# Decoder trunk on one core: score products of row halves and quarters issued in turn, and two gates ahead of the first two branches

## The chip, the core and the metric

The kernel runs on one core of a Trainium2 chip. The metric is device time in microseconds of one execution of the whole program, as the median of several runs. Engines are named as the profile names them: PE (TensorE, matmuls and transposes; PEld are its weight loads), DVE (VectorE), ACT (ScalarE), POOL (GpSimd) and SP (SyncE, which issues the DMAs).

## The reference, cut to what matters

Two layers over one sequence of 256 tokens, width 1024, all float32. Each layer projects the normalised input once, runs four causal mixers (4 query heads of 64 each) on slices of that projection, merges the four results through sigmoid gates, and adds a convolutional feed-forward part.

```python
h = rms_norm(x, norm1_g)
u = h @ w_in
yA = dsa_mixer(...)
yB = moba_mixer(...)
yC = nsa_mixer(...)
yD = swa_mixer(...)
m = sum(sigmoid(gate_n) * (y_n @ w_branch[n]) for n in range(4))
x = x + m @ w_out
x = x + conv_ffn(rms_norm(x, norm2_g), ...)
```

Here `u` holds the columns of the four mixers (2612 in all) and, behind them, the four gates of 1024 columns each. At 256 tokens the mixers are dense masked attention with different masks. A (DSA) has one shared key head and keeps for each query the 64 keys that an indexer scores highest: eight index heads of 32, `I[t,s] = sum_h w[t,h] relu(q_idx[t,h] . k_idx[s])`. B (MoBA) has four key heads and is plain causal here. C (NSA) adds three attentions with a gate each: over 15 compressed blocks (a small MLP makes them), over selected blocks and over a window; at this length the last two are causal attentions with keys of their own. D (SWA) has a window of 128, two key heads and a sink per head.

## The kernel before, in words

**Dense products.** Weights come in chunks of up to 1 MB through three `raw` buffers on SP's queue, in the order of the list `plan` (lines 380 to 435). ACT rounds each piece to `hi` (line 467), DVE computes `lo`, what is left of it (line 477); four buffers each. Activations are split in the same way (`ahi`, `alo`), and a dense product is three PE passes, hi by hi, lo by hi and hi by lo (`macs`, lines 492 to 525), for two tiles of 128 tokens, into the `mm` banks of PSUM. There are four `mm` banks, two `sc` banks (scores) and two `tr` banks (transposes and small products).

**Order of the work.** Everything is unrolled. Each piece of work is a generator ("stream") that asks for an engine, for results and for buffers of rings; `Flow.run` (line 139) is a planner that always lets the stream go on whose request can start first by its clocks, and emits its instructions then. So the order in which each engine's queue holds its instructions is fixed when the program is built, by the costs in `Eng.cost` (lines 180 to 206). For a float32r matmul of n columns line 189 says 0.417 n + 2 ns, doubled while PE's clock in the plan is below 6.7 us. Where two streams can start at the same time the priority decides (a smaller number first; the mixers' are `PRIO`, line 396, A 4, B 19, C 7, D 21, and the main stream's is 40).

**The main stream** (`main`, lines 1233 to 1394) goes through a layer in one order: projections in the column order `PORDER` = A, B, D, C (line 397), then for each branch n = 0 to 3 its gate (two halves of 512 columns, `gate_out` applies the tanh) and its branch product, and then the output projection and the feed-forward part. Between gate 0 and branch 0 stand two small products for C's compression (`hidden`, lines 1019 to 1029), which wait for C's first steps; they run on four column strips of the array with `P.side = 4`. For branches 0 to 2 both gate halves come first and then both branch halves; for branch 3 they alternate. `branch_out` waits for that mixer's result, turned by `y_T` (line 581), which main spawns one branch at a time; `merge` (line 1115) multiplies it with the gate and adds it to `mg`. Gates lie in four places of `slotP` in turn.

**The mixers** (`dsa`, `moba`, `nsa`, `swa`, lines 775 to 1009) are streams of their own that main spawns as their projections end, and they fill PE between main's instructions. One set of buffers, `prep_r` (line 259), is held by one mixer at a time while it normalises, rotates and transposes its queries and keys: A from line 777 to 830, B from 867 to 881, D from 888 to 903, C from 912 to 1005, the last across the compression product. A and B and D ask for it as an ACT request, C as a DVE request. POOL's instructions on `rB`, `rC` and `rD` are the power in each mixer's query norm.

**The score products** that the change is about are the only matmuls that use a part of the array's rows. `attend` (lines 634 to 708) runs for one tile t of 128 queries, nk = 128 (t + 1) keys and four heads of 64: heads 0 and 2 lie in rows 0 to 63, heads 1 and 3 in rows 64 to 127. There are ten attends in a layer (A, B, D, and C twice; t = 0 and 1):

```python
for par in range(2):
    ...
    for hh in range(2):
        te = P.matmul(sc[:, hh * nk:hh * nk + nk], qT[b:b + 64, hh, ...], kT[b:b + 64, ...])
    fl.spawn(attend_max(...), 8)
```

Each half takes one `sc` bank by a request of its own (lines 641 and 645). `indexer` (lines 836 to 864) does the same for the eight index heads of A in four row quarters r4 of 32 rows, one `sc` bank and one request per quarter (lines 840 to 847), followed by a Relu on ACT and two accumulations on DVE.

## Time and profile before

| | us |
|---|---|
| three runs | 877.33, 877.55, 881.88 |
| median of the runs | 877.55 |
| the profiled execution's own time | 881.64 |
| its span, first to last instruction | 879.8 |
| PE in flight | 874.4 |
| DVE busy | 667.9 |
| ACT busy | 526.3 |
| POOL busy | 34.3 |

The profile is one execution; times in its views count from the start of the span. A matmul's time there is its flight: matmuls are pipelined, so the next one starts before the flight of the one before has ended, and the cost of an instruction is read from start to start. The timeline merges neighbours of one kind into one line with their count; most instructions carry line 212, the helper that records them, so groups are told apart by their tiles (output<-inputs).

### The profile page before, as it was taken

The numbers are of one execution on the slowest core, as the hardware profiler recorded it, in microseconds if no ns is written. First come the engines' busy times: TensorE is split into PE (matmuls) and PEld (weight loads), VectorE is DVE, ScalarE is ACT, GpSimd is POOL, SyncE is SP. The second block draws the span as 40 slices with busy tenths as digits, with TensorE's granted clock in tenths as the row PEclk, the third lists the DMA queues.
The fourth block names the chain that finished last, engine by engine and source line by source line (L and its number), as shares of the span: only waits on it lengthen the run. The fifth ranks groups of instructions, "written<-read, shape, count | busy, mean of one in ns | idle before, by whom it ended". The sixth has DMA issues, their size and how long they took to land.

```text
span 879.8 us, 14193 instructions
## 1 busy us (share of the span) xinstructions
PE 874.4 (99%) x5491; PEld 766.2 (87%) x5491; DVE 667.9 (76%) x1301; ACT 526.3 (60%) x895; POOL 34.3 (4%) x31
## 2 busy tenths in 40 slices
PE   9999999999999999999999999999999999999998
PEld 8979887788889999988898888787888999999886
DVE  4779888956768999884457997968476699899642
ACT  5655465555457887764455465646545598888431
POOL 0111002000000000000001111000000000000000
PEclk9999999999999999999999999999999999999999
DMA  7627364235555555555554264542356455565560
GB/s 266 237 87 240 96 239 145 83 127 174 192 176 179 200 191 192 193 168 193 170 172 168 85 205 144 193 144 97 120 184 222 144 192 195 194 201 192 178 215 25
DMA packets 103413, 149.90 MB, mean 170 GB/s; under 512 B 4072, under 2 KB 62258, under 8 KB 103346
## 3 DMA queue, kind: packets, MB, share of 16 engines
q1 hardware_dynamic: 103346, 149.00, 50.6%
q8 instruction: 43, 0.70, 0.3%
q14 instruction: 24, 0.20, 0.1%
HBM read 147.94 MB, written 1.05 MB: 169 GB/s over the span
## 4 chain that ended last, share of the span: by engine, by line
PE 98%; ACT 0%; DMA 0%; SPq 0%; DVE 0%; issue 0%; DVEq 0%
PE mm L212 82%; PE sc L212 8%; PE tr L212 8%; DMA rn<-in_norm_g_dram 0%; ACT f L212 0%; ACT L212 0%; SPq L240 0%; ACT hi L212 0%; DVE x L212 0%; DVEq L1429 0%
## 5 line engine op out<-in xcount | busy, mean ns | idle before, releaser
L212 DVE TENSOR_TENSOR lo<-raw,hi 128x1024 fp32r<-128x1024 f32 (+2 forms) x280 | 328.1, 1177 | 117.2 <-ACT hi L212 113.3
L212 ACT ACTIVATE hi<-raw 128x1024 fp32r<-128x1024 f32 (+2 forms) x280 | 283.3, 1022 | 170.7 <-PE mm L212 143.1
L212 PE MATMUL mm<-hi,ahi 128*128 128x512 f32 (+4 forms) x480 | 178.1, 377 | 0.0
L212 PE MATMUL mm<-hi,alo 128*128 128x512 f32 (+4 forms) x480 | 172.3, 365 | 0.0
L212 PE MATMUL mm<-ahi,hi 128*128 128x256 f32 x640 | 152.3, 279 | 0.0
L212 PE MATMUL mm<-alo,hi 128*128 128x256 f32 x640 | 152.0, 278 | 0.0
L212 PEld LDWEIGHTS mm<-ahi,hi 128*128 128x128 f32 x640 | 120.6, 188 | 0.1
L212 PEld LDWEIGHTS mm<-alo,hi 128*128 128x128 f32 x640 | 120.6, 188 | 0.1
L212 PE MATMUL mm<-lo,ahi 128*128 128x512 f32 (+4 forms) x480 | 118.3, 370 | 0.0
L212 PEld LDWEIGHTS mm<-hi,ahi 128*128 128x128 f32 x480 | 90.7, 189 | 14.9 <-issue 2.7
L212 PEld LDWEIGHTS mm<-hi,alo 128*128 128x128 f32 x480 | 90.8, 189 | 11.2
L212 PEld LDWEIGHTS mm<-lo,ahi 128*128 128x128 f32 x480 | 82.9, 188 | 13.8 <-issue 1.7
L212 PE MATMUL mm<-hi,slotQ 128*128 128x512 f32 x352 | 89.9, 395 | 0.0
L212 PE MATMUL mm<-ahi,lo 128*128 128x256 f32 x640 | 88.1, 278 | 0.0
L212 PEld LDWEIGHTS mm<-ahi,lo 128*128 128x128 f32 x640 | 80.2, 188 | 0.0
L212 PEld LDWEIGHTS mm<-hi,slotQ 128*128 128x128 f32 x352 | 66.1, 188 | 15.3
L212 ACT ACTIVATE f<-f,col 128x256 f32<-128x256 f32 x88 | 48.1, 593 | 14.5 <-DVE f L212 14.0
L212 PE MATMUL mm<-lo,slotQ 128*128 128x512 f32 x176 | 48.7, 395 | 0.0
L212 ACT ACTIVATE f<-f,nmx 128x128 f32<-128x128 f32 (+1 forms) x80 | 35.4, 445 | 9.6 <-DVE nmx L212 9.4
L212 ACT ACTIVATE slotP<-mm,rh 128x512 f32<-128x512 f32 x32 | 20.4, 684 | 33.2 <-PE mm L212 33.0
L212 PE MATMUL sc<-qk 64*128 64x128 f32 (+3 forms) x224 | 39.9, 348 | 0.0
L212 PEld LDWEIGHTS mm<-lo,slotQ 128*128 128x128 f32 x176 | 33.0, 188 | 7.6
(219 smaller groups left out, 1091.7 us busy)
## 6 DMA issues: line engine op xcount, KB each, us to landing
raw<-in_w_up_dram SPq DMA_DIRECT2D x44, 1024.0 KB, 5.0
raw<-in_w_in_dram SPq DMA_DIRECT2D x40, 1024.0 KB, 4.9
raw<-in_w_down_dram SPq DMA_DIRECT2D x20, 1024.0 KB, 4.9
raw<-in_w_out_dram SPq DMA_DIRECT2D x8, 1024.0 KB, 5.2
raw<-in_w_branch_dram SPq DMA_DIRECT2D x6, 1024.0 KB, 5.7
raw<-in_w_in_dram SPq DMA_DIRECT2D x7, 768.0 KB, 6.1
raw<-in_w_in_dram SPq DMA_DIRECT2D x4, 592.0 KB, 4.1
raw<-in_w_in_dram SPq DMA_DIRECT2D x4, 536.0 KB
```

The costliest lines, as they stand in the source:

```text
L212: fn(*a, **k)
```

## The change

- `attend` asks for both score banks in one request and issues the four products with the halves in turn (head 0, 1, 2, 3); both `attend_max` streams start behind the last of them. For the planner a product then costs half (`P.side = 2`).
- `indexer` asks for four banks at once, two `sc` and two `tr`, issues all eight products with the quarters in turn (`P.side = 4`), and then goes through the four Relus.
- The list `SEQ` replaces the loop over branches: gate 0, the compression products, gate 1, branches 0 and 1, gate 2, branch 2, gate 3 and branch 3 by halves. The chunks are loaded in the same order. All four `y_T` streams are spawned ahead of the list.
- `PORDER` becomes A, C, B, D.
- The first gate lands in `mg` itself, the others in four places of `slotP` that are handed on when their merge is done; `merge` is the same pair of instructions, without the addition for the first branch.
- The planner's cost of a float32r matmul becomes 0.446 n + 2 ns.

```diff
--- before.py
+++ after.py
@@ -186,7 +186,7 @@
             if m == "transpose":
                 c = 0.835 * n
             else:
-                c = 0.417 * n + 2 if a[1].dtype == F32R else 1.67 * max(n, free_size(a[1])) + 2
+                c = 0.446 * n + 2 if a[1].dtype == F32R else 1.67 * max(n, free_size(a[1])) + 2
             return c / self.side * (1 if self.flow.clock["PE"] > 6700 else 2)
         ptrs = sum(hasattr(k.get(q), "shape") for q in ("scale", "bias", "accum_out", "scalar"))
         if self.name == "ACT":
@@ -391,10 +391,14 @@
             ap = [f(ap) for f in cut]
         plan.append(Chunk(ap, (nk, n), cut))
 
-    GATES = (0, 1, 2, 3)
-    HID_AT = (0, 1)
+
+    SEQ = [("gate", 0, 0), ("gate", 0, 1), ("hidden", 0, 0), ("hidden", 1, 0), ("gate", 1, 0),
+           ("gate", 1, 1), ("branch", 0, 0), ("branch", 0, 1), ("branch", 1, 0), ("branch", 1, 1),
+           ("gate", 2, 0), ("gate", 2, 1), ("branch", 2, 0), ("branch", 2, 1), ("gate", 3, 0),
+           ("branch", 3, 0), ("gate", 3, 1), ("branch", 3, 1)]
+    FIRST, LAST = [n for op, n, _ in SEQ if op == "branch"][0], SEQ[-1][1]
     PRIO = (4, 19, 7, 21)
-    PORDER = (0, 1, 3, 2)
+    PORDER = (0, 2, 1, 3)
     CH_A, CH_C = [(0, 384), (384, 680)], [(1448, 1832), (1832, 2100)]
     CH_B, CH_D = [(680, 1192), (1192, 1448)], [(2100, 2612)]
     CHS = {0: CH_A, 1: CH_B, 2: CH_C, 3: CH_D}
@@ -408,18 +412,17 @@
         for _, c0, c1 in COLS[2:]:
             for kg in range(2):
                 rows_chunk(wi, 4 * kg, 4 * kg + 4, c0, c1)
-        for n in GATES:
-            for half in range(2):
+        for op, n, half in SEQ:
+            if op == "gate":
                 for kg in range(2):
                     c0 = 2612 + n * D + half * 512
                     rows_chunk(wi, 4 * kg, 4 * kg + 4, c0, c0 + 512)
-                if (n, half) == HID_AT:
-                    for i in range(2):
-                        ap = a["c_cmp_w1"][l, i].rearrange("(c p) h -> p c h", p=128)
-                        plan.append(Chunk(ap, (16, 128), []))
-                if n == GATES[-1]:
-                    rows_chunk(a["w_branch"][l, n], 0, 2, half * 512, half * 512 + 512)
-            if n != GATES[-1]:
+            elif op == "hidden":
+                ap = a["c_cmp_w1"][l, n].rearrange("(c p) h -> p c h", p=128)
+                plan.append(Chunk(ap, (16, 128), []))
+            elif n == LAST:
+                rows_chunk(a["w_branch"][l, n], 0, 2, half * 512, half * 512 + 512)
+            elif half == 0:
                 ap = a["w_branch"][l, n].rearrange("(k p) n -> p k n", p=128)
                 plan.append(Chunk(ap, (2, D), [lambda v, h=h: v[:, :, h * 512:h * 512 + 512] for h in range(2)]))
         for kg in range(2):
@@ -633,21 +636,21 @@
 
     def attend(t, qT, kblk, kT, vfn, scl, mask, y, needs, sink=None, fin=None, gate=None):
         nk = 128 * (t + 1)
-        Sx = sm = None
         rdf = Fut()
         tx = []
+        sxt, sm, *scs = yield "PE", needs, [sx_r, sm_r, sc_r, sc_r]
+        Sx = sxt.rearrange("p (h n) -> p h n", h=H)
+        mx, nmx, den, es, rd = (sm[k] for k in ("mx", "nmx", "den", "es", "rd"))
+
+        P.side = 2
+        for hh in range(2):
+            for par in range(2):
+                b = 64 * par
+                te = P.matmul(scs[par][:, hh * nk:hh * nk + nk], qT[b:b + 64, hh, t * 128:t * 128 + 128],
+                              kT[b:b + 64, kblk(2 * hh + par), :nk], start=True, stop=True)
+        P.side = 1
         for par in range(2):
-            if par == 0:
-                sxt, sm, sc = yield "PE", needs, [sx_r, sm_r, sc_r]
-                Sx = sxt.rearrange("p (h n) -> p h n", h=H)
-                mx, nmx, den, es, rd = (sm[k] for k in ("mx", "nmx", "den", "es", "rd"))
-            else:
-                sc, = yield "PE", [], [sc_r]
-            b = 64 * par
-            for hh in range(2):
-                te = P.matmul(sc[:, hh * nk:hh * nk + nk], qT[b:b + 64, hh, t * 128:t * 128 + 128],
-                              kT[b:b + 64, kblk(2 * hh + par), :nk], start=True, stop=True)
-            fl.spawn(attend_max(t, sc, te, par, Sx, nk, mask, scl, sink, mx, tx), 8)
+            fl.spawn(attend_max(t, scs[par], te, par, Sx, nk, mask, scl, sink, mx, tx), 8)
         yield "DVE", [_Pair(tx)], []
         tm = V.tensor_scalar(nmx, mx, -1.0, None, op0=ALU.mult)
         for h in range(H):
@@ -837,15 +840,21 @@
         nk = 128 * (t + 1)
         mask = tri[:, 256 - nk:]
         ac = acc[t]
+
+        rgs = [sc_r, sc_r, tr_r, tr_r]
+        bks = yield "PE", needs, rgs
+        P.side = 4
+        for g in range(2):
+            for r4 in range(4):
+                tm = P.matmul(bks[r4][:, g * nk:g * nk + nk], iqT[32 * r4:32 * r4 + 32, g, t * 128:t * 128 + 128],
+                              ikT[32 * r4:32 * r4 + 32, 0, :nk], start=True, stop=True)
+        P.side = 1
+        td = 0.0
         for r4 in range(4):
-            sc, rl = yield "PE", needs, [sc_r, rl_r]
-            for g in range(2):
-                te = P.matmul(sc[:, g * nk:g * nk + nk], iqT[32 * r4:32 * r4 + 32, g, t * 128:t * 128 + 128],
-                              ikT[32 * r4:32 * r4 + 32, 0, :nk], start=True, stop=True)
-            yield "ACT", [te], []
-            te = A.activation(rl[:, :2 * nk], sc[:, :2 * nk], AF.Relu)
-            sc_r.give(sc, te)
-            td = te
+            rl, = yield "ACT", [tm], [rl_r]
+            te = A.activation(rl[:, :2 * nk], bks[r4][:, :2 * nk], AF.Relu)
+            rgs[r4].give(bks[r4], te)
+            td = max(td, te)
             for g in range(2):
                 yield "DVE", [td], []
                 h = 4 * g + r4
@@ -1112,17 +1121,13 @@
             mm_r.give(ps[t], tq)
         f.t = tq
 
-    def merge(mg, ps, rg, te, gate, gf, half, i, old, f):
+    def merge(mg, ps, rg, te, gate, gf, half, more, old, f):
         hs = slice(half * 512, half * 512 + 512)
         for t in range(NT):
-            if i == 0:
-                yield "DVE", [te, gf], []
-                tq = V.scalar_tensor_tensor(mg[:, t, hs], gate[:, t, :], 1.0, ps[t], op0=ALU.add, op1=ALU.mult)
-            else:
-                yield "DVE", [te, gf], []
-                tq = V.scalar_tensor_tensor(gate[:, t, :], gate[:, t, :], 1.0, ps[t], op0=ALU.add, op1=ALU.mult)
+            yield "DVE", [te, gf], []
+            tq = V.scalar_tensor_tensor(gate[:, t, :], gate[:, t, :], 1.0, ps[t], op0=ALU.add, op1=ALU.mult)
             rg.give(ps[t], tq)
-            if i:
+            if more:
                 yield "DVE", [tq] + old, []
                 tq = V.tensor_tensor(mg[:, t, hs], mg[:, t, hs], gate[:, t, :], op=ALU.add)
         f.t = tq
@@ -1279,18 +1284,51 @@
                     fl.spawn(proj_out(banks[i], te, rstd[2 * l], r1f, [(proj[n][:, :, c0 - base:c1 - base], 0, c1 - c0)], f), 3)
                     if c1 == CHS[n][-1][1]:
                         mixer(n, f)
-            gts = None
-            mT = None
+            gts = mT = None
             mf = [Fut() for _ in range(4)]
-            merged = [[Fut(), Fut()] for _ in range(4)]
-            def branch_out(i, half, yT, ytf, pc_, gate, gf):
+            merged = [[], []]
+            places = [([], o) for o in range(0, 4096, 1024)]
+            gates, yTs, shared = {}, {}, {}
+
+            def gate_of(n, half):
+
+                nonlocal gts
+                ps = yield "PE", [], [mm_r] * NT
+                if n == FIRST:
+                    old, dst = [], mg[:, :, half * 512:half * 512 + 512]
+                else:
+                    if gts is None:
+                        gts = one.tile([128, 8 * 512], F32, name="slotP")
+                    old, o = places.pop(0)
+                    dst = gts[:, o:o + 1024].rearrange("p (t n) -> p t n", t=NT)
+                f = Fut()
+                gates[n, half] = dst, f, None if n == FIRST else o
+                for kg in range(2):
+                    ch = next(it)
+                    te = yield from macs(ch, ch.pieces, ps, hget, hfut, 4 * kg, kg == 0, kg == 1)
+                fl.spawn(gate_out(ps, te, rh[l], rhf, old, dst, f), 3)
+
+            def branch_out(n, half):
                 nonlocal mT
+                yT, ytf = yTs[n]
+                if n == LAST:
+                    pc_ = next(it).pieces[0]
+                else:
+                    if half == 0:
+                        shared[n] = next(it)
+                    pc_ = shared[n].pieces[half]
+                gate, gf, o = gates[n, half]
                 rg = sc_r if half == 0 and all(f.t is not None for f in yf) else mm_r
                 ps = yield "PE", [ytf], [rg] * NT
                 te = yield from macs(None, [pc_], ps, lambda v, k: yT[0][v][:, k, :], lambda k: [], 0, True, True)
-                f = merged[i][half]
-                fl.spawn(merge(mg, ps, rg, te, gate, gf, half, i, [merged[i - 1][half]] if i else [], f), 3)
-                if i == 3:
+                if half == 1:
+                    y_r.give(yT[0], te)
+                f, old = Fut(), merged[half][-1:]
+                merged[half].append(f)
+                if n != FIRST:
+                    places.append(([f], o))
+                fl.spawn(merge(mg, ps, rg, te, gate, gf, half, n != FIRST, old, f), 3)
+                if n == LAST:
                     if half == 0:
                         mt = one.tile([128, 14 * 512], F32R, name="slotQ")
                         mT = (mt[:, 0:KD * S].rearrange("p (k s) -> p k s", k=KD),
@@ -1298,33 +1336,18 @@
                     for j in range(2):
                         k0 = 4 * half + 2 * j
                         fl.spawn(rows_T(mg[:, :, 128 * k0:128 * k0 + 256], [f], mT, k0, mf[2 * half + j], scale=0.5), 2)
-                return te
-
-            for i, n in enumerate(GATES):
-                gate, gf = [], []
-                yT, ytf = [], Fut()
-                fl.spawn(y_T(ys[n], yf[n], yT, ytf), 2)
-                for half in range(2):
-                    ps = yield "PE", [], [mm_r] * NT
-                    if gts is None:
-                        gts = one.tile([128, 8 * 512], F32, name="slotP")
-                    o = 1024 * ((2 * i + half) % 4)
-                    gate.append(gts[:, o:o + 1024].rearrange("p (t n) -> p t n", t=NT))
-                    gf.append(Fut())
-                    for kg in range(2):
-                        ch = next(it)
-                        te = yield from macs(ch, ch.pieces, ps, hget, hfut, 4 * kg, kg == 0, kg == 1)
-                    fl.spawn(gate_out(ps, te, rh[l], rhf, [merged[i - 2][half]] if i > 1 else [], gate[half], gf[half]), 3)
-                    if (n, half) == HID_AT:
-                        for j in range(2):
-                            yield from hidden(j, next(it), hid)
-                    if i == 3:
-                        te = yield from branch_out(i, half, yT, ytf, next(it).pieces[0], gate[half], gf[half])
-                if i < 3:
-                    ch = next(it)
-                    for half in range(2):
-                        te = yield from branch_out(i, half, yT, ytf, ch.pieces[half], gate[half], gf[half])
-                y_r.give(yT[0], te)
+
+            order = [n for op, n, half in SEQ if op == "branch" and half == 0]
+            for i, n in enumerate(order):
+                yTs[n] = [], Fut()
+                fl.spawn(y_T(ys[n], yf[n], *yTs[n]), 2)
+            for op, n, half in SEQ:
+                if op == "gate":
+                    yield from gate_of(n, half)
+                elif op == "hidden":
+                    yield from hidden(n, next(it), hid)
+                else:
+                    yield from branch_out(n, half)
             ps2 = []
             xf = [Fut(), Fut()]
             h2f = [Fut() for _ in range(KD)]
```

## Rows read from the trace of the kernel before

**Rows 1.** Page, part 1: PE and the other engines, busy and share of span

```profile
PE 874.4 (99%) x5491; PEld 766.2 (87%) x5491; DVE 667.9 (76%) x1301; ACT 526.3 (60%) x895; POOL 34.3 (4%) x31
```

**Rows 2.** Page, part 4: the chain that ended last, by engine

```profile
PE 98%; ACT 0%; DMA 0%; SPq 0%; DVE 0%; issue 0%; DVEq 0%
```

**Rows 3.** Waits of PE over the span: us in total, times, longest

```profile
PE sc L212 <- DVE f L212: 1.0, 1, 1.0
PE sc L212 <- DMA rn<-in_norm_g_dram: 0.4, 1, 0.4
```

**Rows 4.** Windows: length, busy us of the engines (instructions), PEclk, DMA share, GB/s

```profile
20.00:180.00 160.00, 160.00 (x954) 132.19 (x953) 137.25 (x386) 90.66 (x192) 15.75 (x10) 1.00 0.47 159
180.00:270.00 90.00, 90.00 (x477) 76.49 (x476) 56.01 (x74) 46.48 (x64) 0.69 (x1) 1.00 0.48 164
470.00:620.00 150.00, 149.94 (x904) 123.15 (x902) 126.98 (x372) 84.51 (x182) 13.00 (x7) 1.00 0.43 145
```

**Rows 5.** Instructions on the tile sc: min/median/max ns, first and last start, forms

```profile
L212 PE MATMUL sc<-qk x224: 270/374/480, 48.2 to 611.2; 64*128 64x128 f32 x40, 64*128 64x256 f32 x40, 32*128 32x128 f32 x16, 32*128 32x256 f32 x16
```

**Rows 6.** Timeline of PE, layer 0 (start, flight, instruction, count): both halves, and neighbours

```profile
81.61 0.39 PE L212 MATMUL mm<-hi,ahi 128*128 128x512 f32 x1
81.84 0.40 PE L212 MATMUL mm<-hi,alo 128*128 128x512 f32 x1
82.16 0.72 PE L212 MATMUL sc<-qk 64*128 64x128 f32 x8
82.82 0.96 PE L212 MATMUL mm<-lo,ahi 128*128 128x512 f32 x3
...
88.52 1.14 PE L212 MATMUL sc<-qk 64*128 64x256 f32 x8
...
103.64 1.49 PE L212 MATMUL sc<-qk 64*128 64x256 f32 x8
105.05 0.50 PE L212 MATMUL mm<-hi,ahi 128*128 128x512 f32 x1
105.39 0.40 PE L212 MATMUL mm<-hi,alo 128*128 128x512 f32 x1
```

**Rows 7.** Timeline of PE: one row half alone

```profile
159.87 1.13 PE L212 MATMUL sc<-qk 64*128 64x256 f32 x4
...
600.82 0.71 PE L212 MATMUL sc<-qk 64*128 64x128 f32 x4
```

**Rows 8.** Timeline of PE: quarters of the indexer, alone, same quarter twice, two quarters

```profile
48.23 1.57 PE L212 MATMUL sc<-qk 32*128 32x128 f32 x8
...
53.55 1.13 PE L212 MATMUL sc<-qk 32*128 32x256 f32 x4
...
488.50 1.13 PE L212 MATMUL sc<-qk 32*128 32x256 f32 x8
```

**Rows 9.** Timeline of PE, layer 1: the compression product on four column strips

```profile
552.91 1.07 PE L212 MATMUL mm<-raw,kr 128*15 128x128 f32 x32
```

**Rows 10.** Timelines of ACT and PE, layer 0: branch results turned and used

```profile
111.71 0.50 PE L212 MATMUL mm<-hi,yhi 128*128 128x512 f32 x1
...
124.36 0.60 ACT L212 ACTIVATE yhi<-tr 128x512 fp32r<-128x512 f32 x1 [3.05 <-PE tr L212]
...
151.22 0.48 PE L212 MATMUL mm<-hi,yhi 128*128 128x512 f32 x1
```

**Rows 11.** Timeline of POOL, layer 0: the norms of B, C and D

```profile
80.96 3.81 POOL L212 TENSOR_TENSOR rB<-rB,mhalf 128x16 f32<-128x16 f32 x1 [25.55 <-DVE rB L212]
108.34 1.64 POOL L212 TENSOR_TENSOR rC<-rC,mhalf 128x8 f32<-128x8 f32 x1 [23.58 <-DVE rC L212]
...
142.82 3.26 POOL L212 TENSOR_TENSOR rD<-rD,mhalf 128x12 f32<-128x12 f32 x1 [9.22 <-DVE rD L212]
```

**Rows 12.** Timeline of ACT, layer 1: B's first step; today's third projection

```profile
492.65 1.06 ACT L212 ACTIVATE rt<-slotQ 128x1024 f32<-128x1024 f32 x1
...
498.01 1.27 ACT L212 ACTIVATE slotQ<-mm,rstd 128x512 f32<-128x512 f32 x2 [2.26 <-PE mm L212]
```

## The prediction

> **What bounds the kernel now.** I read the page's busy shares first, then its chain, then PE's waits. TensorE (PE) is in flight for 874.4 us of a span of 879.8 [rows 1]; 98% of the chain that ended last is PE itself [rows 2]; in the whole span PE waited for somebody twice, 1.0 and 0.4 us [rows 3]. The granted clock is 1.00 in each stretch that I asked for, which is the 2.4 GHz level [rows 4]. So nothing is to be uncovered first: time falls only if PE's own work falls, and rises if the new order makes PE wait. VectorE (DVE) is the next engine: in the stages of the four mixers, 20:180 and 470:620, it is busy for 137.25 of 160 and 126.98 of 150 us [rows 4].
>
> **Terms of the sum.** The profiled execution took 881.64 us (span 879.8); the median of the runs shown is 877.55, so it was one of the longer ones. I work the difference out from the profile and take it off the median.
>
> *The score products.* There are 112 (20 attends of 4 heads, 4 indexer blocks of 8), and each leaves two matmul records: 224, from 48.2 to 611.2 us [rows 5]. In the timeline they stand in 40 groups. The next instruction starts about 0.07 us before a group's flight ends (82.16 plus 0.72, against 82.82 [rows 6]), so a group's cost is its flight less 0.07:
> - Four records on one row half: 0.64 us with 128 columns (flight 0.71), 1.06 with 256 (1.13) [rows 7].
> - Eight records, both halves, issued as four and four by lines 647 to 650: 0.65 us with 128 columns, 1.07 with 256 [rows 6]. Two halves that meet cost what one costs. They meet today only where the planner happened to put the second half right behind the first; where its bank came late they meet partly (103.64 to 105.05, 1.41 us [rows 6]).
> - One quarter of the indexer: 1.06 us with 256 columns; two quarters that meet, eight records, also 1.06; two blocks of the same quarter do not overlap, 1.50 [rows 8].
> - Going in and out: the matmul ahead of a group gives way after 0.32 us instead of 0.23, and the one behind keeps PE for 0.34 [rows 6]. That is 0.2 per group beside dense matmuls, less beside transposes; I take 0.18.
>
> Before, attends: 27 groups. Seven eights of 128 columns at 0.65, two eights of 256 at 1.07, four late ones (1.42, 1.60, 1.26, 1.26), six fours at 0.64 and eight fours at 1.06: 24.5 us, with 27 x 0.18 = 4.9 makes 29.4. After: each attend is one group with its halves in turn, 10 x 0.65 + 10 x 1.07 + 20 x 0.18 = 20.8. **Saved: 8.6 us.**
>
> Before, indexers: 13 groups. Two mixed ones (1.50 each), five fours of 128 (0.64), five fours of 256 and the pair of quarters (1.06 each): 12.5 us, with 13 x 0.18 makes 14.9. After: four groups; if all four quarters run together a group costs what one quarter costs, 2 x 0.64 + 2 x 1.06 + 4 x 0.18 = 4.1. **Saved: 10.8 us.** No row shows four row groups at once. Bounds: only two at once gives 2 x (8 x 0.112 + 0.2) + 2 x (8 x 0.216 + 0.2) + 0.7 = 6.8, saved 8.1; no overlap gives 12.0, saved 2.9 (0.112 and 0.216 are a record's step: 0.64 and 1.06 less 0.2, over four). More than full overlap has no source. I take full overlap: two quarters already cost what one does, and the nearest thing with four, the compression product on four column strips, sends 32 records through in 1.07 us of flight [rows 9].
>
> *What else the edits touch.* The pace in the cost table changes only the order: PE's 512-column step is 0.23 us [rows 6], the old line gives 0.2155, the new one 0.2304. The first gate lands in `mg` itself and its merge is the same instruction in place: nothing added on ACT or DVE. The DMAs are the same, in another order on SP's queue; their cover is a DMA share of 0.43 to 0.48 in these stretches [rows 4], and the one wait for a transfer that PE has today is 0.4 us [rows 3].
>
> *Banks.* An attend asks for both score banks at once and an indexer block for all four score and transpose banks, until ACT has read each. Transposes of other mixers queue behind that; dense matmuls, which use the other four banks, cover it. With the cover gone it costs the blocks' own length, at most the 4 x 1.06 us that the quarters of a block take today, for four blocks 17 us; I take nothing, the lower end, since with 160.00 of 160 us busy PE has always found dense work beside the mixers [rows 4].
>
> *The order of branches.* Gate 1 moves ahead of branch 0, so DSA's result gains a gate of cover: 96 matmuls of 0.23, 22 us. Branch 1 then follows branch 0 at once. Today MoBA's result is turned at 124.36 and used at 151.22, 27 us later [rows 10]. Branches 2 and 3 come up earlier by what PE saves, some 10 us a layer; work that DVE does not finish by then spreads into 180:270, where it has 56.01 of 90 busy [rows 4]. I take nothing; the bounds are in the second rival.
>
> Sum: 8.6 + 10.8 = 19.4 us off PE's own work, 877.55 - 19.4 = 858.2; rounded up for the small stalls of a reshuffled order, **859 us**.
>
> **Rivals.**
> *DVE gives part of it back.* It is busy for 264 of the mixers' 310 us, 85%; with 19 us less that is 91% of 291 [rows 4]. If that is more than its queue can do without lateness, splits of weights come late and about half is lost: 868 us. Against: only the branches have due times, and the stage behind has room.
>
> *MoBA stands behind NSA.* This one ends on the other side. One buffer (`prep_r`) is handed from mixer to mixer. POOL's rows show today's order in layer 0: B's norm at 80.96, C's at 108.34, D's at 142.82 [rows 11]. With C projected second, C can ask before B. In layer 1 B takes the buffer at 492.65, when A leaves it, while today's third projection lands at 498.01 [rows 12]; with C's and B's columns ahead, the new third one is some 3 us more dense work, less some 4 to 5 of indexer: about 4 us after A's release there. If C takes the buffer, it keeps it until the compression product, which stays behind gate 0 and today ends as branch 0 starts, at 111.71 [rows 10], and 31 us beyond (to D's norm). B would start near 134 (111.7 - 6 of indexer savings + 31, less B's own work of today), and its result, 25 us later at best (43 today, from 80.96 to 124.36), near 159; branch 1 would be due at 111.7 - 6 + 22 of gate 1 + 9 of branch 0 = 137. Of those 22 us I take some 9 as filled by mixers' PE work: 13 lost per layer, 26 in all, **884 us**. It decides from 9.7 us lost per layer on; less than that leaves a smaller gain. For: layer 1's handing over. Against: requests go by start time first, and B's (ACT) can win over C's (DVE, the busier).
>
> *Starts in program order only.* Were it so, a product's second record would hold back the next product's first, and a group would take 5 steps instead of 4 with halves, 9 with quarters: 10 x (0.112 + 0.216) + 2 x 5 x (0.112 + 0.216) = 6.6 us less saved, 865. Today's rows speak against it: issued four and four, the halves still ran side by side [rows 6]. The Trainium skill, in TensorE: Matmul & The Clock Gate, Part 3 (Packing small matmuls), says matmuls are "pc-monotone in start AND end — strict FIFO, no reordering". The groups at 82.16 and 88.52 differ from that sentence, so this rival gets little.
>
> **How the numbers follow.** Forecast 0.54; DVE's half 0.12; program order 0.06; MoBA late 0.28, of which a small loss that leaves a gain of over 0.5% 0.03, one that cancels it 0.10, the full one 0.15. The bound of 0.5%, 4.4 us, is about what a measurement of this kernel can tell. Faster 0.75, same 0.10, slower 0.15. Low end: 859 less the 4.5 us by which the runs shown differ, 854. High end: quarters not overlapping (867), DVE's half (868) and the cancelled gain, 878; above it lie the slower cases.
>
> **What would show it.** Right: 24 groups of score records instead of 40, eight near 0.65 and 1.07 us and sixteen near 0.64 and 1.06, and PE still without waits. Wrong: sixteen records in 1.1 or 1.9 us (pairs only); PE idle ahead of the second branch, with POOL's rows in the order C before B (the second rival); PE waiting for `lo` with DVE over 91% (the first).

## The result, and the profile of the changed kernel

869.12 us (median of 5, 864.62 to 870.07) against 878.27 for the kernel before (5 runs, 877.33 to 882.23): a ratio of 0.9878, interval 0.9851 to 0.9905. That is 1.2% faster, more than the 0.5% that the prediction takes as the bound. The profiled execution took 864.62 us, its span 862.8; that of before 881.64 and 879.8. Times and ratios here and below are of runs in one state; only e3 has others, 937.1 to 940.5 us, left out here, and the 937 us that an expectation names is its median with them.

The page of the changed kernel, parts 1 and 4 (they answer to [rows 1, 2]):

```profile
PE 856.4 (99%) x5491; PEld 755.6 (88%) x5491; DVE 666.6 (77%) x1297; ACT 529.1 (61%) x899; POOL 35.7 (4%) x31
...
PE 91%; DVE 7%; POOL 1%; issue 0%; ACT 0%; DVEq 0%
```

PE's busy time fell by 18.0 us and the span by 17.0, with as many PE instructions (x5491): the same matmuls overlap more. The chain now names DVE for 7%, but PE is in flight for 99%, so these are steps beside PE's work. PE's waits (us in total, times, longest) answer to [rows 3]:

```profile
PE sc L212 <- DVE f L212: 1.0, 1, 1.0
PE tr L212 <- DVE qr L212: 0.5, 2, 0.3
```

The windows, with the columns of [rows 4]. PE is as full as before, at a granted clock of 1.00 (2.4 GHz):

```profile
20.00:180.00 160.00, 159.80 (x1010) 134.52 (x1009) 141.22 (x393) 97.36 (x200) 16.04 (x9) 1.00 0.50 168
180.00:270.00 90.00, 89.78 (x494) 76.95 (x493) 59.65 (x79) 50.30 (x71) 0.69 (x1) 1.00 0.50 169
470.00:620.00 150.00, 149.67 (x901) 122.84 (x900) 126.11 (x359) 89.21 (x184) 13.54 (x6) 1.00 0.45 151
```

The timeline of PE, layer 0, answers to [rows 6] (two halves) and [rows 8] (quarters; half of their records stand under `tr`, whose banks they borrow):

```profile
43.86 0.38 PE L212 MATMUL sc<-qk 32*128 32x128 f32 x2
43.88 0.38 PE L212 MATMUL tr<-qk 32*128 32x128 f32 x2
44.08 0.28 PE L212 MATMUL sc<-qk 32*128 32x128 f32 x2
44.09 0.28 PE L212 MATMUL tr<-qk 32*128 32x128 f32 x2
...
44.52 0.50 PE L212 MATMUL mm<-hi,ahi 128*128 128x512 f32 x1
...
52.06 0.48 PE L212 MATMUL sc<-qk 32*128 32x256 f32 x2
...
53.13 0.97 PE L212 MATMUL mm<-lo,ahi 128*128 128x512 f32 x3
...
70.61 0.72 PE L212 MATMUL sc<-qk 64*128 64x128 f32 x8
71.25 0.74 PE L212 MATMUL mm<-lo,ahi 128*128 128x512 f32 x2
...
81.98 1.14 PE L212 MATMUL sc<-qk 64*128 64x256 f32 x8
83.05 0.50 PE L212 MATMUL mm<-hi,ahi 128*128 128x512 f32 x1
```

Every attend is now one group of eight, 0.64 us with 128 columns (70.61 to 71.25) and 1.07 with 256 (one of the ten of 256 takes 1.14). An indexer block is one group of sixteen, in four steps of four records, one on each quarter, that start within 20 ns: 0.66 us (43.86 to 44.52) and 1.07 (52.06 to 53.13), as long as one quarter took alone. POOL's norms in layer 0, with those of [rows 11]: MoBA's (B) still comes before NSA's (C), and C's 7 us earlier than before:

```profile
79.02 4.01 POOL L212 TENSOR_TENSOR rB<-rB,mhalf 128x16 f32<-128x16 f32 x1 [26.77 <-DVE rB L212]
101.02 1.64 POOL L212 TENSOR_TENSOR rC<-rC,mhalf 128x8 f32<-128x8 f32 x1 [17.98 <-DVE rC L212]
...
134.01 2.27 POOL L212 TENSOR_TENSOR rD<-rD,mhalf 128x12 f32<-128x12 f32 x1 [9.43 <-DVE rD L212]
```

**What does not fit.** The forecast was 859. The profiled run lies 5.6 us above it, and the others of that measurement lie 4 to 5.5 us higher again. The median is inside the range, but the gain, 9.2 us between the medians, is about half of what was forecast (18.6).

### The profile page after: what moved, and what is told of

It is laid out like the page before. It is cut to its first block, busy times and chain, and to the rows that moved or that the text cites. A ratio compares the mean times of both kernels' runs of the same rounds, so it can differ in the third digit from the quotient of the medians.

```text
span 862.8 us, 14190 instructions
## 1 busy us (share of the span) xinstructions
PE 856.4 (99%) x5491; PEld 755.6 (88%) x5491; DVE 666.6 (77%) x1297; ACT 529.1 (61%) x899; POOL 35.7 (4%) x31
## 4 chain that ended last, share of the span: by engine, by line
PE 91%; DVE 7%; POOL 1%; issue 0%; ACT 0%; DVEq 0%
PE mm L212 76%; PE tr L212 8%; PE sc L212 6%; DVE lo L212 2%; DVE acc L212 2%; POOL rB L212 1%; DVE m L212 1%; DVE f L212 1%; DVE rt L212 0%; POOL rqA L212 0%; DVE rB L212 0%; DVE qr L212 0%; ACT hi L212 0%; DVE qk L212 0%; ACT rt L212 0%
## 5 line engine op out<-in xcount | busy, mean ns | idle before, releaser
L212 ACT ACTIVATE qk<-f,col 128x256 f32<-128x256 f32 x88 | 39.2, 495 | 0.0
L212 DVE SCALAR_TENSOR_TENSOR f<-f,col,f 128x254 f32<-128x254 f32 x88 | 38.4, 477 | 0.0
```

Of the source, the lines that this page charges most:

```text
L212: fn(*a, **k)
```

## The experiments

Two questions: which part of the change carries the gain, and where 10 us of the 19.4 went. All runs stand in one table, "kept" and "put back" told by its columns. *Scores*: the new attend and index block. *Pace*: the cost table's 0.446 (new) or 0.417 (old). *PORDER*: the order of the projections (1 is B, 2 is C, 3 is D). *Loop*: the new sequence of gates and branches, or the old one. Then the median, its ratio to before in the same measurement (whose medians are 881.0 to 881.3 from e1 on), the length of the mixers' stage (first projection matmul to first up matmul) and of the up stage (first up matmul to the last one of hi by hi) in layers 0 and 1, from the profiled run, and the order in which the buffer is handed on; that A comes first is the kernel's order, the rest is read from POOL's rows. The mixers' columns are the cleaner measure of the change: the up stage has two lengths of its own, for a reason that comes further down.

| kernel | scores | pace | PORDER | loop | us | ratio [95%] | mixers 0, 1 | up 0, 1 | handed on 0, 1 |
|---|---|---|---|---|---|---|---|---|---|
| before | old | old | 0132 | old | 878.27 | 1 | 249.1, 248.1 | 124.3, 119.7 | ABCD, ABDC |
| after | new | new | 0213 | new | 869.12 | 0.9878 [0.9851, 0.9905] | 240.3, 238.9 | 124.9, 120.0 | ABCD, ABCD |
| e1 | new | new | 0213 | new | 869.24 | 0.9877 [0.9851, 0.9903] | 239.6, 238.9 | 125.1, 124.4 | ABCD, ABCD |
| e2 | new | old | 0132 | old | 876.38 | 0.9955 [0.9934, 0.9976] | 257.0, 239.0 | 120.2, 119.7 | ABDC, ABCD |
| e3 | old | new | 0213 | new | 928.16 | 1.0536 [1.0478, 1.0593] | 261.8, 272.1 | 124.9, 124.4 | ACBD, ACBD |
| e7 | old | new | 0123 | new | 881.76 | 1.0027 [1.0011, 1.0043] | 249.9, 247.6 | 124.9, 120.0 | ABCD, ABCD |
| e8 | new | old | 0123 | old | 879.80 | 1.0002 [0.9980, 1.0023] | 246.7, 250.4 | 124.2, 119.7 | ABCD, ABDC |
| e11 | new | new | 0132 | old | 872.89 | 0.9916 [0.9888, 0.9943] | 241.5, 242.8 | 124.7, 124.4 | ABCD, ABDC |
| e9 | new | new | 0213 | old | 867.69 | 0.9847 [0.9825, 0.9869] | 240.7, 238.8 | 124.5, 124.4 | ABCD, ABCD |
| e10 | new | old | 0213 | new | 888.39 | 1.0089 [1.0069, 1.0109] | 249.1, 257.2 | 124.4, 119.7 | ABCD, ACBD |
| e4 | as after, smalls late | | | | 863.73 | 0.9805 [0.9784, 0.9826] | 240.0, 238.9 | 120.5, 124.4 | ABCD, ABCD |
| e5 | e4, rstd late too | | | | 858.63 | 0.9760 [0.9734, 0.9787] | 240.0, 238.9 | 120.3, 119.7 | ABCD, ABCD |
| e6 | before, smalls late | | | | 877.55 | 0.9971 [0.9955, 0.9988] | 250.2, 248.1 | 120.2, 119.7 | ABCD, ABDC |

### The parts of the change

**e2, the scores alone, and e3, the rest alone.** e2 puts the diff's hunks of `attend` and the index block into the kernel before; e3 takes the same hunks out of the changed one. e3's is e2's backwards:

```diff
-        for par in range(2):
...
+        sxt, sm, *scs = yield "PE", needs, [sx_r, sm_r, sc_r, sc_r]
...
-        for r4 in range(4):
-            sc, rl = yield "PE", needs, [sc_r, rl_r]
...
+        rgs = [sc_r, sc_r, tr_r, tr_r]
+        bks = yield "PE", needs, rgs
```

> The kernel before with the halves and quarters in turn (attend and indexer as in the changed kernel) and nothing else: old pace, old order of projections, gates and branches. Theory 1 (PE's work decides, the order is worth nothing by itself): 24 groups of score records, about 25 us with the ways in and out instead of 44, and a span some 17 to 19 us below that of the kernel before at equal pace of the up stages, 861 to 863 us where one layer is at 117.8 ns. Rival (the new order is needed to cover the mixers): PE waits ahead of the first branches and half of the saving or less is left, a span of 870 us or more.

> The changed kernel with attend and indexer as they were before: the new order of projections, gates and branches and the new pace alone. Theory 1: the 40 or so groups of score records are back at about 44 us, and the span is within 3 us of the kernel before at equal pace of the up stages, 877 to 883 us where one layer is at 117.8 ns. Rival (the order brings a part of the gain): 870 us or less.

Neither half carries the gain by itself: e2's span is 874.2 us where its first theory has 861 to 863, e3's 920.9 where its first has 877 to 883. e3's two runs, 922.68 and 933.63 us, average 47 us above before (881.34): here the second rival happens. POOL's rows of e3, layer 0:

```profile
79.80 2.54 POOL L212 TENSOR_TENSOR rC<-rC,mhalf 128x8 f32<-128x8 f32 x1 [28.64 <-DVE rC L212]
126.22 1.64 POOL L212 TENSOR_TENSOR rkC<-rkC,mhalf 128x8 f32<-128x8 f32 x1 [0.34 <-DVE rkC L212]
138.64 3.80 POOL L212 TENSOR_TENSOR rB<-rB,mhalf 128x16 f32<-128x16 f32 x1 [10.79 <-DVE rB L212]
```

The windows of e3 behind the first branch, in layers 0 and 1 (columns as in [rows 4]):

```profile
130.00:180.00 50.00, 41.94 (x254) 33.15 (x253) 42.28 (x154) 26.20 (x80) 6.07 (x2) 0.93 0.18 60
...
590.00:640.00 50.00, 42.43 (x201) 34.13 (x198) 33.84 (x130) 19.79 (x69) 4.28 (x2) 0.62 0.13 43
```

C takes the buffer first and B's norm comes at 138.64 instead of 80.96. PE first idles, and then the granted clock falls to the lower of its two levels (0.50 of 2.4 GHz, 1.2 GHz); 0.62 is the mean of a window with both. Shorter windows in layer 1 show the order:

```profile
590.00:595.00 5.00, 2.05 (x16) 1.34 (x12) 5.00 (x22) 0.00 (x0) 2.02 (x1) 0.86 0.66 210
595.00:605.00 10.00, 8.37 (x35) 6.81 (x36) 8.61 (x31) 6.12 (x24) 0.00 (x0) 0.50 0.00 0
```

In e2 the place is another: D has the buffer before C in layer 0 (POOL's rD at 109.79, rC at 127.27), so NSA's compression product starts at 125.3 us where the gate ahead of it ends at 98. The mixers' stage takes 257.0 us, though layer 1, with A, B, C, D, shows the whole gain (239.0). Here too the clock falls with the idling, as the window of e2 between these times shows:

```profile
100.00:130.00 30.00, 22.52 (x152) 17.27 (x151) 20.94 (x73) 13.24 (x38) 4.94 (x2) 0.54 0.27 82
```

**e7, e3 with B projected first; e8, e2 with C before D.** Both ask whether the handing over is all. e7's line (e8's is the same, from `(0, 1, 3, 2)`):

```diff
-    PORDER = (0, 2, 1, 3)
+    PORDER = (0, 1, 2, 3)
```

> The changed kernel with attend and indexer as before (as in the run that took 937 us) but with the projections in the order A, B, C, D, so that B asks for the shared buffer ahead of C in both layers. Theory 1 (the 937 us came from the buffer going to C before B, and the order of gates and branches is worth nothing by itself): within 3 us of the kernel before at equal pace, 877 to 884 us. Rival (gate 1 ahead of branch 0, or the new pace, made the loss): 900 us or more.

> The kernel before with halves and quarters in turn and the projections in the order A, B, C, D; gates, branches and pace as before. The buffer is handed on as in the kernel before (B, C, D in layer 0, B, D, C in layer 1). Theory 1 (the score products bring all of the gain if the buffer is handed on in time; the run with the scores alone lost most of it because D took the buffer before C in layer 0): 17 to 19 us below the kernel before at equal pace, 860 to 866 us. Rival (the new order of gates is needed): 870 us or more.

e7 gives e3's loss back, 928.2 to 881.8: without the new products, pace and sequence together are worth nothing (ratio 1.0027). e8 was a miss: with A, B, C, D in layer 0 it should have shown the scores' gain, and it was no faster than before. Its windows around the first gates:

```profile
90.00:120.00 30.00, 26.75 (x197) 20.88 (x196) 25.03 (x80) 16.53 (x42) 1.64 (x1) 0.89 0.51 176
510.00:570.00 60.00, 54.98 (x344) 44.15 (x343) 48.59 (x149) 31.86 (x80) 6.81 (x3) 0.86 0.39 123
```

PE is idle for 3.3 and 5.0 us there and partly at the lower clock; its longest waits are 2.0 and 1.9 us for `kr`, which DVE writes for the mixers. So the order of handing over is not all. e8 differs from the changed kernel in pace, sequence and `PORDER`; the next three part them.

**e9, the change with the old loop; e10, with the old pace; e11, scores and pace in the kernel before.** e9 takes the sequence out (`for n in GATES` in place of `for op, n, half in SEQ`), and with it the first gate's place in `mg` and the early `y_T` streams. e10 takes the changed line out, e11 puts it into e2:

```diff
-                c = 0.446 * n + 2 if a[1].dtype == F32R else ...
+                c = 0.417 * n + 2 if a[1].dtype == F32R else ...
```

> The changed kernel with the old loop over branches (gate 0, compression products, branch 0, gate 1, branch 1, ...) and all else as changed: halves and quarters in turn, projections A, C, B, D, new pace. The buffer is handed on as A, B, C, D in both layers, as in the changed kernel. Theory A (once PE is faster, the mixers' results and C's first steps come too late for branch 0 right behind gate 0, and gate 1 is what covers them): PE waits ahead of the first branches, 5 to 10 us per layer, a span of 872 us or more. Theory B (the handing on of the buffer is what decides, and the place of gate 1 is worth nothing): as the changed kernel, 863 to 867 us.

> The changed kernel with the planner's old pace of a float32r matmul (0.417 n + 2), all else as changed. The buffer then goes to C before B in layer 1, and to B first in layer 0. Theory (the pace matters only through that race): layer 0 as in the changed kernel, layer 1 loses 15 to 30 us with PE waiting ahead of the second branch, a time of 882 to 900 us. Rival (PE's order by the right pace is worth something everywhere, or nothing at all): layer 0 longer too, or 864 to 870 us in all.

> The kernel before with halves and quarters in turn and the new pace, nothing else: projections A, B, D, C and the old loop over branches. The buffer is handed on as in the kernel before (B, C, D in layer 0, B, D, C in layer 1). Theory P (the right pace alone lets the gain through, because DVE's queue then holds its instructions in the order in which PE's results come): as the changed kernel, 860 to 870 us. Theory Q (the projection of C ahead of B is needed too, since the compression product behind gate 0 waits for C's first steps and D takes the buffer first in layer 1): PE waits ahead of that product, 8 to 20 us, 873 us or more.

The sequence is worth nothing that shows: e9's stages are e1's within 1.1 us. The pace is worth 19 us in this kernel (888.39 against 869.12): with the old line the changed kernel is slower than before. In layer 1 it goes over to the second rival, as POOL's rows of e10 show:

```profile
515.42 1.64 POOL L212 TENSOR_TENSOR rC<-rC,mhalf 128x8 f32<-128x8 f32 x1 [29.44 <-DVE rC L212]
...
572.93 3.88 POOL L212 TENSOR_TENSOR rB<-rB,mhalf 128x16 f32<-128x16 f32 x1 [18.27 <-DVE nmx L212]
```

The window of that stage in e10, with 8.8 us in which PE is not busy:

```profile
470.00:630.00 160.00, 151.19 (x898) 123.59 (x897) 128.73 (x371) 86.50 (x179) 14.38 (x7) 0.95 0.43 138
```

Layer 0 keeps A, B, C, D and takes 249.1 us all the same, 9.5 more than e1's. So both halves of e10's expectation came true, its theory in layer 1 and its rival in layer 0, where it is as in e8: from 90 to 110 us PE is busy for 15.67 of 20, with a longest wait of 2.0 us for `kr`.

e11 has the scores and the pace: layer 0 shows nearly the whole gain (241.5), layer 1, where D is still handed the buffer before C, 4 us less (242.8 against 238.8 in e9, which differs from it in `PORDER` alone). Its time falls between its two theories: the wait ahead of the compression product that the second one names is there, but it takes 1.9 us, not 8 to 20. Against e2, which differs in the pace alone, the two mixers' stages together are 11.7 us shorter (484.3 against 496.0), but the time falls by only 3.5: its up stages are 9.2 us longer, 4.7 of that in layer 1, where the pace has a part in it (further down). So the new pace helps in one stage and costs in another.

### Where the rest went

**e1, the changed kernel again**, for a second profile.

> The changed kernel once more, nothing edited. Theory 1 (the saving of PE's own work is all there, and what differs from run to run is the pace of the up-projection): in the profile the 256-column matmuls of a layer's up stage step by either 113.3 or 117.8 ns, nothing between, which is 94.1 or 97.8 us for the stage from its third pair of chunks on; the span follows the number of layers at the slower pace, 862.8 us where it is one layer, 866.5 where it is two, 859 where it is none. Theory 2 (the runs scatter for another reason): the up stages are as in the first profile (117.8 and 113.3) and the span is nevertheless near 867 us, or the other way round.

The same kernel, the mixers' stages alike to 0.7 us, and a span of 866.6 instead of 862.8: the difference is layer 1's up stage, 124.4 against 120.0, as the first theory has it. Windows of 65 us inside the up stages of layers 0 and 1, of the changed kernel's first profile:

```profile
300.00:365.00 65.00, 65.00 (x554) 65.00 (x553) 59.22 (x82) 51.71 (x81) 0.00 (x0) 1.00 0.58 195
...
710.00:775.00 65.00, 65.00 (x575) 65.00 (x575) 61.89 (x86) 54.44 (x87) 0.00 (x0) 1.00 0.62 206
```

The window in layer 1 of e1:

```profile
710.00:775.00 65.00, 65.00 (x555) 65.00 (x554) 59.51 (x83) 52.64 (x84) 0.00 (x0) 1.00 0.58 190
```

The same matmuls of 256 columns, no wait, the clock 1.00, and yet 575 of them in one run and 555 in another: 113.3 or 117.8 ns from start to start, and nothing between. The timelines show where the paces part, at two transposes of `rstd` that the planner puts between them. PE's timeline in the first profile:

```profile
681.12 0.28 PE L212 MATMUL mm<-alo,hi 128*128 128x256 f32 x1
681.44 0.43 PE L212 MATMUL tr<-cst,rstd 128*128 128x128 f32 x2
681.63 0.37 PE L212 MATMUL mm<-ahi,hi 128*128 128x256 f32 x1
...
682.52 0.28 PE L212 MATMUL mm<-alo,hi 128*128 128x256 f32 x1
682.63 0.28 PE L212 MATMUL mm<-ahi,hi 128*128 128x256 f32 x1
```

The same place in e1's timeline:

```profile
680.16 0.28 PE L212 MATMUL mm<-alo,hi 128*128 128x256 f32 x1
680.48 0.43 PE L212 MATMUL tr<-cst,rstd 128*128 128x128 f32 x2
680.67 0.36 PE L212 MATMUL mm<-ahi,hi 128*128 128x256 f32 x1
...
681.58 0.28 PE L212 MATMUL mm<-alo,hi 128*128 128x256 f32 x1
681.70 0.28 PE L212 MATMUL mm<-ahi,hi 128*128 128x256 f32 x1
```

Both come 0.32 us after the matmul ahead of them; behind them a step is 113 ns in the one and 118 in the other, and stays so to the stage's end. In layer 0 most profiles change from 114 to 118 at three transposes of `smalls` (the next layer's small vectors); e3 and e7 do so at `rstd` already, and e2 stays at 113.5 behind both.

How far behind the matmul ahead the `rstd` transposes start follows from the pace in the cost table. PE's timelines of before and of e2 (old pace) and of e11 (e2 with the new pace, nothing else), in this order:

```profile
698.08 0.62 PE L212 MATMUL mm<-ahi,lo 128*128 128x256 f32 x4
698.53 0.38 PE L212 MATMUL tr<-cst,rstd 128*128 128x128 f32 x2
...
692.54 0.62 PE L212 MATMUL mm<-ahi,lo 128*128 128x256 f32 x4
693.00 0.38 PE L212 MATMUL tr<-cst,rstd 128*128 128x128 f32 x2
...
685.15 0.28 PE L212 MATMUL mm<-alo,hi 128*128 128x256 f32 x1
685.47 0.43 PE L212 MATMUL tr<-cst,rstd 128*128 128x128 f32 x2
```

In the first two the last of the four matmuls starts 0.34 us into its line, and the transposes 0.11 us after it; in e11 they start 0.32 us after. All five kernels with the old pace (before, e2, e6, e8, e10) have 0.11 us, and their layer 1 keeps 113 ns, 119.7 us. All with the new pace have 0.32 us except e5, and of those seven five (e1, e3, e4, e9, e11) have 118 ns behind it in layer 1, two (after, e7) 113.

**e4 and e5, the transposes moved; e6, the same in the kernel before.** e4 and e6 spawn `smalls` at the last pair of the up stage instead of ahead of the loop; e5 also plans `rb_stream`'s two transposes 1.5 us later:

```diff
-            if l + 1 < DEPTH:
-                fl.spawn(smalls(l + 1, te[1, 1]), 2)
             for c in range(2, KF, 2):
+                if l + 1 < DEPTH and c == KF - 2:
+                    fl.spawn(smalls(l + 1, t), 2)
...
-        tb, = yield "PE", [rf], [tr_r]
+        yield "POOL", [rf], []
+        tb, = yield "PE", [rf.t + 1500], [tr_r]
```

> The changed kernel with the loads and the three small transposes for layer 1's columns started behind the last pair of up chunks of layer 0 instead of behind the first. In both profiles the up stage of layer 0 steps by 113 ns until those three transposes come by (275.55 us in the kernel before) and by 117.8 behind them, and layer 1, which has none, stays at 113.3. Theory 1 (the transposes push the stream of matmuls and weight loads into the slower pace, which then holds): layer 0's up stage steps by 113.3 ns, 94.1 instead of 97.8 us, and the span falls by 3.7 us against the changed kernel. Rival (the pace has to do with the layer, its data or buffers): 117.8 ns in layer 0 as before, no difference.

> The changed kernel with the small transposes of layer 0 late, as in the run before, and besides with the two rstd transposes of both layers planned 1.5 us later, so that PE no longer stands waiting for them in the first up product (317 to 322 ns there, behind which layer 1 stepped by 113.3 in one profile and by 117.8 in two). Theory 1 (a short wait at interposed transposes decides which of the two paces the up stage takes): both layers at 113.3 ns in the profile, span near 859 us, every run near 860.5, and the runs closer together than 2 us. Rival (the pace in layer 1 is chance, whatever stands there): one or two layers at 117.8, times of 863 to 868 us.

> The kernel before with the small transposes of layer 0 late and nothing else. Theory 1 (two paces of the up stage explain the two clusters of the kernel before, near 881.5 and near 877.3): layer 0 at 113.3 ns, every run near 877.3, 4 us below the usual run of the kernel before. Rival (the clusters have another cause): both clusters again.

e4 shortens layer 0's up stage to 120.5 us, e5 layer 1's too. e5's windows:

```profile
300.00:365.00 65.00, 65.00 (x574) 64.82 (x573) 61.48 (x87) 54.21 (x87) 0.00 (x0) 1.00 0.60 190
710.00:775.00 65.00, 65.00 (x576) 65.00 (x575) 61.80 (x87) 53.68 (x85) 0.00 (x0) 1.00 0.62 202
```

e5's two transposes in PE's timeline, which now start 0.11 us after the matmul ahead:

```profile
676.64 0.28 PE L212 MATMUL mm<-alo,hi 128*128 128x256 f32 x1
676.75 0.38 PE L212 MATMUL tr<-cst,rstd 128*128 128x128 f32 x2
```

e5's five runs lie within 1.5 us (857.74 to 859.19) and e6's twelve within 1.7 (876.34 to 878.07), where before, in the same measurement, showed runs near 877.3 and near 881.5. e5 is the fastest kernel of all here, 858.63 us, 2.4% under before.

## Why the prediction was right, and which step was off

**What bounds the kernel.** Right: PE is full before and after, and the time fell because PE's work in the mixers' stages did.

**The score products.** Right in size. After: 24 groups, the attends' and indexers' flights less overlaps sum to 20.6 us and the ways in and out to 4.6, together 25.2, where the steps gave 20.8 + 4.1 = 24.9; before came to 44.3 by the same count. Saved: 19.1 (19.4 predicted). The mixers' stages got shorter by 8.8 and 9.2 us. Full overlap of four quarters was right (0.66 and 1.07 us), but no row had shown it: it was a choice that came out; with pairs only (8.1 us for 10.8) the sum would have been 861.

**Costed at nothing.** The banks: right, as far as PE's 1.5 us of waits show. The order of branches: right, e9. The DMAs: right, PE waits for none in the first profile and for 1.0 us in e1's. The pace: wrong to put at nothing. It changes the order alone, but that order lets the gain through (e10 without it is 888.4) and also moves the transposes of the up stage.

**The rivals.** The time alone would have pointed at a rival: 869.12 is next to the 868 of the first and 865 of the third. The rows rule both out. *DVE gives part of it back*: refuted. It is busier (141.22 of 160 us, [rows 4] had 137.25), and PE waits 1.5 us in all. *MoBA stands behind NSA*: it did not happen in the changed kernel, but its place was right, and a nearby plan falls into it (e3 in both layers, e10 in layer 1). Its price, 13 us a layer, holds for one layer only: against e7 the mixers' stages of e3 are 11.9 us longer in layer 0 and 24.5 in layer 1, where the clock stayed low for longer (both with the old score products). That B's request can win over C's held in the changed kernel; with the old score products it lost in both layers (e3), with the old pace in layer 1 (e10). *Starts in program order only*: refuted; a group of eight in turn takes 4 steps (1.07 us), not 5. The two records of a product need not both start before the next product's first: the four quarters start within 20 ns (the rows at 43.86 and 43.88), and the second records come one step later (44.08). The Trainium skill's sentence in TensorE: Matmul & The Clock Gate, Part 3, "strict FIFO, no reordering", does not describe these records; the measurement decides.

**The step that was off**: "rounded up for the small stalls of a reshuffled order, 859", and ahead of it "The pace in the cost table changes only the order", put at nothing. The stalls are small (PE's waits, 1.5 us). What came in their place is the step of the up stage's matmuls, which the prediction did not look at, and it acts twice. First, the 877.55 that 19.4 was taken from is, by its time, a run in which both up stages keep 113 ns: e6, where they do in its profile, has a median of 877.55 too. Most runs of before are near 881.5, with layer 0 at 118 (124.3 us, the profiled one among them). Second, the changed kernel has 118 in layer 0 and, it seems, in most runs goes over to 118 in layer 1 as well: with the old pace the transposes there start 0.11 us behind a matmul and the stage takes 119.7 us; with the new pace they start 0.32 us behind it. e1 against e5 prices both: spans of 866.6 and 856.0, of which the up stages are (125.1 + 124.4) - (120.3 + 119.7) = 9.5. At equal step the forecast holds: e6 to e5 is 877.55 - 858.63 = 18.9 us for 19.4, and the two first profiles, both with 118 in layer 0 and 113 in layer 1, differ by 17.0. But the 859 was forecast for the changed kernel, which takes 869; e5 is another kernel. That the time still lies in the range is its width: 878, its upper end, stood for other losses. That the runs of after near 869 have both layers at 118 is shown by e1's profile alone (868.36); the other runs left none.

**Open.** Why the same instructions have two paces, and what at the transposes decides between them, is not settled: a start 0.32 us behind stands ahead of both outcomes in layer 1, and in layer 0 transposes of `smalls` at the same distances have left 113.5 ns in e2 and 118 in e8. The change with PORDER alone put back, in its own loop, was not tried.

## What to carry to other kernels

Products on different row groups should be issued in turn, all into banks asked for at once: here four quarters cost what one does. Work that is saved on the bounding engine arrives only if the order planned by hand still holds, so the planner's costs have to be those of the trace, and the order in which a shared buffer is handed on belongs in the list of things to look at. A corrected cost moves work in every stage: here it helped in one and cost in another, so compare all stages. Ahead of a sum, take its base from runs whose stages have the same lengths: here two groups of runs 4 us apart were two paces of one stage.

## What the runs showed of the hardware that was not expected

- Matmuls of 256 columns in an alternation with weight loads have two stable paces, 113.3 and 117.8 ns, at a granted clock of 1.00 and without waits. In all profiles here a stage keeps its pace until transposes (two or three) are put between; the difference is 4.1 to 4.7 us per up stage.
- Four row groups overlap fully even for products of two records each: sixteen records in 0.66 us (128 columns) and 1.07 us (256).
- A planning loss is paid twice: in e3's layer 1 PE is busy for 2.05 of 5 us from 590, and from 595 to 605 the granted clock is 0.50; in e2 it is 0.54 on average from 100 to 130 us, where PE is busy for 22.52.
